# A two-layer decoder in fp32 on one core: the second layer's first query weight is split inside the last layer norm, its value weights later, and four memory pools wait per tile

## The chip, the cores and the metric

The kernel runs on one core of a Trainium2 chip. The metric is device time in microseconds (us) for one execution; less is better. The core has a matrix engine (TensorE, PE in the profile, with its weight loads as PEld), a vector engine (VectorE, DVE), an activation engine (ScalarE, ACT), a general engine (GpSimd, POOL), and a queue that issues most of the loads (SyncE, SP). Each engine executes its own instructions strictly in the order in which they were put there and waits for the others through semaphores.

## What is computed

The input is 512 tokens of 1024 numbers. Layer A is latent attention (8 heads), layer B attention over a window of 128 tokens (16 query heads, 4 key and value heads). After each comes a layer norm, then a multilayer perceptron (MLP) with squared relu and a second layer norm:

```python
for l in range(DEPTH):                       # DEPTH = 2: layer A, then layer B
    if l < n_a:
        y = _mla(x, mla_w_in[l], ...)
    else:
        k_band, v_band = _shared_kv(x, kv_w_shared)
        y = _swa(x, swa_w_q[b], swa_sinks[b], swa_w_o[b], k_band, v_band, rel_bias)
    x = _layernorm(alpha * x + y, ln_mix_g[l], ln_mix_b[l])
    x = _layernorm(alpha * x + _mlp(x, mlp_w_up[l], mlp_w_down[l]), ln_mlp_g[l], ln_mlp_b[l])
```

All of it is fp32. The kernel gets fp32 accuracy from a faster matmul by **splitting** each operand into a high part (a rounding copy) and a low part (the rest), and by adding three products: high by high, high by low, low by high.

## The kernel before, in words

**Stages.** Pools of on-chip memory are opened and closed one after the other: `mla` (layer A's attention), then `xtok` (which stays open), `mlp0`, `swa` (layer B's attention), `mlp1`. Each new pool uses memory that a closed one has left. A tile in such memory may be written only when the work on what lay there is done; with the plain form of `tile_pool` the first use of a new pool waits for all tiles of the old one.

**Weights.** All weights form one list, `stream`, in the order in which the matmuls need them. Each is loaded into one of two `raw` buffers (SP queue, line 140), split on ACT into `wh` (L76) and on DVE or POOL into `wl` (L79), in rings of four tiles each. `weights(name)` hands out the next one and prepares others ahead, up to `state["hold"]`; `prepare(n)` raises that limit by n and prepares at once. Layer B's part of the list begins `w_k`, `w_k`, `w_sq` 0, `w_v`, `w_v`, `w_sq` 1 and so on: two weights for keys, one for the first two query heads, two for values.

**The end of layer A's attention.** `TokMajor.finish` multiplies the heads' outputs by `w_o`, eight weight tiles. The first four give columns 0 to 511 and the last four columns 512 to 1023 of each of the four token tiles `xs[t]`. The residual input is loaded into `xs` (tag `x`) when the `xtok` pool opens (L1105). Each finished token tile goes through `layer_norm` (L391 to L400: aggregate the statistics, `v`, a power on POOL at L375, then two passes over x, L396 and L400).

**The start of layer B.** The last layer norm of the MLP hands its result to `x2`: for each token tile eight PE transposes into two banks (`tr`, two buffers, L411), then an ACT copy `xth` and a DVE subtraction `xtl` of each bank. `begin` computes keys and the first queries in two halves of 256 tokens. In the first half, PE runs `w_k` 0, `w_k` 1, the transposes of token tile 2, four of eight steps of `w_sq` 0, the transposes of token tile 3, the other four steps; in the second half all three again, over token tiles 2 and 3. The keys are split by small 64x256 operations, `skh` on ACT (L1125) and `skl` on DVE (L1126).

**Layer B's heads.** `run_steps` walks 16 heads. For each, PE computes scores; DVE adds the bias and takes the maximum (L1199); ACT takes exponentials (L1207); POOL scales by the reciprocal sum (`p`, L1214 and L1216); PE transposes (L1227, L1229); ACT and DVE split the transposed tile (`pth`, `ptl`); PE multiplies by the values. Per pair of heads the result `o` is split on ACT (`oh`) and POOL (`ol`, L79) for the output matmul with `w_so`. The order in which operations of different heads stand on ACT, DVE and POOL is set by a scheduler, which takes times and priorities into account; the order of PE and of most loads is that of the program (`pe(...)`, `keep_in_program_order`).

Of the kernel before, what the change touches and what calls it, by code (L numbers as in the profile page):

```python
# [8 lines left out]
F32 = mybir.dt.float32  # L9
F32R = mybir.dt.float32r  # L10
# [38 lines left out]
def build(tc, nc, io, out):  # L49
    with ExitStack() as top:  # L50
# [45 lines left out]
        def pin(ins):  # L96

            if pinned[0]:
                pe(ins)
# [286 lines left out]

        def layer_norm(t, gb, dst):

            x = xs[t]
            mv = sp.tile([P, 2], F32, tag="mv", bufs=4, name=nm("mv"))  # L390
            pin(nc.vector.bn_aggr(mv, stats[t]))  # L391
            stats[t] = None
            v = sp.tile([P, 1], F32, tag="v", bufs=8, name=nm("v"))
            pin(nc.vector.tensor_scalar(v, mv[:, 1:2], LN_EPS, None, ALU.add))  # L394
            r = rsqrt_of(v)
            pin(nc.vector.scalar_tensor_tensor(x, x, mv[:, 0:1], gb[:, 0, :], ALU.subtract, ALU.mult))  # L396
            n = 2 if dst is None and t == NT - 1 else 1
            for i in range(n):
                c = slice(i * D // n, (i + 1) * D // n)
                pin(nc.vector.scalar_tensor_tensor(x[:, c], x[:, c], r, gb[:, 1, c], ALU.mult, ALU.add))  # L400
                if dst is None:
                    nc.sync.dma_start(out[t * P : (t + 1) * P, c], x[:, c])
# [22 lines left out]
        class TokMajor:  # L425
# [24 lines left out]

            def finish(self, gb=None, dst=None, early=None):

# [6 lines left out]
                if gb is not None:  # L459
                    gb = gb()  # L460
                    ws = [weights(self.name) for _ in range(4)]
                    for t in range(NT):
# [11 lines left out]
                        with tc.high_priority():  # L474
                            layer_norm(t, gb, dst)
                        if early:
# [71 lines left out]
        def begin(src, chunks):  # L548


            state["hold"] = len(stream)
            ws = [weights(name) for name, _ in chunks]
            for half_ in range(2):
                cols = slice(half_ * 256, half_ * 256 + 256)
                for i, (_, evac) in enumerate(chunks):
# [8 lines left out]
                    if half_ == 0 and i == 1:  # L564
                        with tc.high_priority():
                            src.turn(NT - 2)


# [68 lines left out]
        def mlp(src, gb, dst, mp):  # L637
# [157 lines left out]
            class Hidden:  # L795
# [6 lines left out]
                def of(self, p, k, cols):  # L802
                    n = ((2, 1), (4, 0))[cols.start // 256][k // 4]
                    return b.fac[n][:, p, k % 4, cols.start % 256 : cols.start % 256 + P]

            if dst is not None:
                state["hold"] = first_sq
            TokMajor(Hidden(), add_last, "down").finish(gb, dst, dst and (0, 0, 0, 1))


        ed = dr.tile([SQH, BANDW], F32, name="ed")
        band = dr.tile([SQH, P, 256], F32, name="band")
        with tc.tile_pool(name="mla", bufs=1) as mp:
            const = mp.tile([P, C_ALL], F32, name="const")
            with tc.issue_after(small.ins):
# [3 lines left out]
            sin = const[:, C_SIN : C_SIN + 256].rearrange("p (t d) -> p t d", t=NT)  # L819
            ckv_h = mp.tile([P, 2, S], F32R, name="ckv_h")  # L820
            ckv_l = mp.tile([P, 2, S], F32R, name="ckv_l")
            khh = mp.tile([P, S], F32R, name="khh")
            kll = mp.tile([P, S], F32R, name="kll")
            cq_h = mp.tile([P, 3, S], F32R, name="cq_h")
            cq_l = mp.tile([P, 3, S], F32R, name="cq_l")
            qrot = mp.tile([P, NT, 512], F32, name="qrot")

# [272 lines left out]

        xtok = top.enter_context(tc.tile_pool(name="xtok", bufs=1))

# [4 lines left out]
        x2 = Feat()  # L1107
        with tc.tile_pool(name="mlp0", bufs=1) as mp:
            mlp_pool[0] = mp
# [6 lines left out]

        with tc.tile_pool(name="swa", bufs=1) as mp:
            khh = [mp.tile([P, S], F32R, name=nm("skh")) for _ in range(SKVH)]
# [163 lines left out]
        gb = lambda: load_gb(io["ln_mix_g"][1], io["ln_mix_b"][1])  # L1282
        with tc.tile_pool(name="mlp1", bufs=1) as mp:
            mlp_pool[0] = mp
# [113 lines left out]
```

## Time and profile before

| what | us |
|---|---|
| median of three runs | 1015.11 (1014.65 to 1015.61) |
| the profiled execution, its own time | 1012.41 |
| its span, first to last instruction | 1010.6 |
| PE busy | 991.6 (98%) |
| DVE busy | 767.4 (76%) |
| ACT busy | 555.5 (55%) |
| POOL busy | 232.7 (23%) |

The profiled execution took 1.8 us more than its span (start and end of the program) and 2.7 us less than the median. A row of the timeline gives the start, the duration, the engine, the line of the program, the operation with output and inputs, and in brackets how long the engine had been idle before it and which operation ended that. In a row "wh<-raw", for example, a split's high part is made from a loaded weight. A busy PE is not necessarily PE at its peak; the clock that was granted to it is given for each stretch of time (1.00 is full speed).

### The profile page before, as it was taken

Reading aid. Unit: us, or ns where it says so; the run is one execution under the profiler, and the core shown is the slowest. Engines: PE = TensorE matmul, PEld = TensorE weight load, DVE = VectorE, ACT = ScalarE, POOL = GpSimd, SP = SyncE. Lnnn points to the kernel's source line nnn. Section 1 sums busy time; section 2 is a strip of 40 time slices with the busy share of each in tenths; the row PEclk is TensorE's granted clock in tenths of the full one; section 3 lists DMA queues with packets and bytes.
Section 4 is the critical chain, followed back from the end, with each engine's and each line's share of the span. In section 5 each row is a group of like instructions: output and inputs, shape, how many; then the busy total and the mean of one; then the engine's idle time right before and its main releaser. Section 6 shows DMA issues by size and latency. Waiting matters only on the chain. (4 is left out here: it accounts for less than half of the span.)

```text
span 1010.6 us, 15862 instructions
## 1 busy us (share of the span) xinstructions
PE 991.6 (98%) x6148; PEld 893.4 (88%) x6148; DVE 767.4 (76%) x1231; ACT 555.5 (55%) x847; POOL 232.7 (23%) x204
## 2 busy tenths in 40 slices
PE   8999999999999999999999999999999999999996
PEld 8888887999999999998889888889998999998986
DVE  5588866889769769886695578589896886888756
ACT  5456643467637637646146688446663764665620
POOL 0231101312212211210014674223122032122002
PEclk9999999999999999999999999999999999999999
DMA  7431108397978977963232212247698798798332
GB/s 244 142 99 43 63 22 260 65 218 218 200 167 221 185 178 194 232 117 105 104 104 95 84 65 74 85 124 199 179 217 190 165 221 170 166 265 150 84 125 83
DMA packets 60246, 149.55 MB, mean 148 GB/s; under 512 B 5211, under 2 KB 9740, under 8 KB 60172
## 3 DMA queue, kind: packets, MB, share of 16 engines
q0 software_dynamic: 24320, 58.73, 32.4%
q1 hardware_dynamic: 35852, 89.82, 26.2%
q8 instruction: 48, 0.79, 0.3%
q14 instruction: 26, 0.21, 0.1%
HBM read 146.41 MB, written 4.22 MB: 149 GB/s over the span
## 5 line engine op out<-in xcount | busy, mean ns | idle before, releaser
L103 PE MATMUL mm<-wh,fac 128*128 128x512 f32 (+1 forms) x944 | 293.0, 386 | 0.0
L76 ACT ACTIVATE wh<-wq 128x1024 fp32r<-128x1024 f32 x164 | 173.6, 1060 | 189.5 <-PE mm L103 130.3
L79 DVE TENSOR_TENSOR wl<-wq,wh 128x1024 fp32r<-128x1024 f32 x164 | 199.2, 1221 | 72.6 <-ACT wh L76 71.3
L103 PE MATMUL mm<-xth,wh 128*128 128x256 f32 (+1 forms) x936 | 245.0, 290 | 0.0
L103 PE MATMUL mm<-xth,wl 128*128 128x256 f32 (+1 forms) x808 | 235.0, 291 | 1.5 <-DVE wl L79 1.2
L103 PEld LDWEIGHTS mm<-wh,fac 128*128 128x128 f32 x944 | 176.3, 188 | 35.4 <-DVE fac L79 0.6
L103 PE MATMUL mm<-xtl,wh 128*128 128x256 f32 (+1 forms) x680 | 198.9, 293 | 0.4 <-DVE xtl L79 0.4
L103 PE MATMUL mm<-wl,fac 128*128 128x512 f32 (+1 forms) x472 | 182.6, 387 | 0.0
L103 PEld LDWEIGHTS mm<-xth,wh 128*128 128x128 f32 x936 | 170.3, 192 | 3.0
L103 PEld LDWEIGHTS mm<-xth,wl 128*128 128x128 f32 x808 | 154.8, 192 | 4.4 <-DVE wl L79 2.1
L76 ACT ACTIVATE wh<-raw 128x1024 fp32r<-128x1024 f32 (+4 forms) x85 | 84.3, 997 | 96.4 <-PE mm L103 62.7
L188 POOL DMA_DIRECT2D wq<-in_up x64 | 77.6, 1222 | 246.7 <-DVE wl L79 180.3
L103 PEld LDWEIGHTS mm<-xtl,wh 128*128 128x128 f32 x680 | 130.2, 191 | 3.8 <-DVE xtl L79 0.8
L79 DVE TENSOR_TENSOR wl<-raw,wh 128x1024 fp32r<-128x1024 f32 (+3 forms) x64 | 75.4, 1189 | 40.4 <-ACT wh L76 40.4
L103 PEld LDWEIGHTS mm<-wl,fac 128*128 128x128 f32 x472 | 88.8, 188 | 17.0 <-DVE wl L79 0.5
L188 POOL DMA_DIRECT2D wq<-in_down x48 | 42.0, 874 | 204.8 <-DVE wl L79 201.4
L375 POOL TENSOR_TENSOR rs<-v,half 128x1 f32<-128x1 f32 x24 | 28.8, 1199 | 194.0 <-DVE v L394 156.8
L79 POOL TENSOR_TENSOR wl<-raw,wh 128x1024 fp32r<-128x1024 f32 (+2 forms) x21 | 43.8, 2089 | 79.6 <-ACT wh L76 79.6
L103 PE MATMUL mm<-wh,oh 128*128 128x512 f32 x128 | 51.0, 398 | 0.5 <-ACT wh L76 0.5
L103 PE MATMUL mm<-wh,ol 128*128 128x512 f32 x128 | 50.2, 392 | 1.0 <-POOL ol L79 1.0
L103 PE MATMUL mm<-wl,oh 128*128 128x512 f32 x128 | 50.0, 390 | 0.8 <-DVE wl L79 0.8
L532 DVE TENSOR_TENSOR x<-mm,x 128x512 f32<-128x512 f32 (+1 forms) x53 | 35.6, 676 | 13.8 <-PE mm L103 13.5
(218 smaller groups left out, 1844.3 us busy)
## 6 DMA issues: line engine op xcount, KB each, us to landing
wq<-in_up POOLq DMA_DIRECT2D x64, 512.0 KB, 8.5
wq<-in_down POOLq DMA_DIRECT2D x48, 512.0 KB, 7.9
wq<-in_up SPq DMA_DIRECT2D x32, 512.0 KB, 5.7
raw<-in_down SPq DMA_DIRECT2D x28, 512.0 KB, 6.4
wq<-in_down SPq DMA_DIRECT2D x24, 512.0 KB, 8.2
raw<-in_up SPq DMA_DIRECT2D x16, 512.0 KB, 6.3
raw<-in_w_o SPq DMA_DIRECT2D x8, 512.0 KB, 3.2
raw<-in_w_sq SPq DMA_DIRECT2D x8, 512.0 KB, 3.2
```

The source lines that it names most:

```text
L76: high = nc.scalar.activation(dst_h, src, AF.Copy)
L79: low = (engine or nc.vector).tensor_sub(dst_l, src, f32(dst_h))
L103: pe(nc.tensor.matmul(dst, st, mv, start=first and i == 0, stop=last and i == len(pairs) - 1, **kw))
L188: nc.gpsimd.dma_start(half(a, jp), chunk(*more, jp), accum_op=ALU.add)
L375: nc.gpsimd.tensor_tensor(r, v, half, ALU.pow)
L532: nc.vector.tensor_add(xs[t][:, c], b, xs[t][:, c])
```

## The change

- **The first query weight of layer B** (`w_sq` 0) is no longer loaded into a `raw` buffer. Ahead of the last matmul of layer A's MLP it is loaded into a tile of 128x4x256 numbers with the tag `a12`, a quarter of the MLP's hidden activations that is no longer used by then. Its split is called inside `layer_norm` of the last token tile, between the power on POOL and the first pass over x (`within`), instead of behind that norm.
- **The value weights** come later: `begin` no longer raises the limit at its start. The first `w_v` is prepared behind the first half (`prepare(1)`), the second when it is wanted; the limit is raised at the end.
- **Pools** `xtok`, `mlp0`, `swa` and `mlp1` are opened with `reuse_waits="tile"`: a new tile waits for the old tiles whose memory it takes, not for the whole closed pool.
- **The order of tiles in `mla`** is another, so that other memory lies at the pool's start, where `xtok` will be: `qrot`, `cq_h`, `cq_l` (rotated queries and query latents) come first, in place of `const` (mask and rotary tables), `ckv_h`, `ckv_l` and the rotated keys.

```diff
-        def layer_norm(t, gb, dst):
+        def layer_norm(t, gb, dst, within=None):
...
             r = rsqrt_of(v)
+            if within:
+                within()
             pin(nc.vector.scalar_tensor_tensor(x, x, mv[:, 0:1], gb[:, 0, :], ALU.subtract, ALU.mult))
...
-                            layer_norm(t, gb, dst)
+                            layer_norm(t, gb, dst, within if t == NT - 1 else None)
...
         def begin(src, chunks):
-            state["hold"] = len(stream)
             ws = [weights(name) for name, _ in chunks]
...
+                if half_ == 0:
+                    prepare(1)
+            state["hold"] = len(stream)
...
+            within = None
             if dst is not None:
                 state["hold"] = first_sq
-            TokMajor(Hidden(), add_last, "down").finish(gb, dst, dst and (0, 0, 0, 1))
+                early = mp.tile([P, 4, 256], F32, tag="a12", bufs=1, name=nm("w_sq"))
+                fetchers[first_sq](early.rearrange("p a b -> p (a b)"))
+                within = lambda: prepare(1)
+            TokMajor(Hidden(), add_last, "down").finish(gb, dst, dst and (0, 0, 0, 0), within)
...
         with tc.tile_pool(name="mla", bufs=1) as mp:
+            qrot = mp.tile([P, NT, 512], F32, name="qrot")
+            cq_h = mp.tile([P, 3, S], F32R, name="cq_h")
+            cq_l = mp.tile([P, 3, S], F32R, name="cq_l")
+            ckv_h = mp.tile([P, 2, S], F32R, name="ckv_h")
+            ckv_l = mp.tile([P, 2, S], F32R, name="ckv_l")
             const = mp.tile([P, C_ALL], F32, name="const")
...
-        xtok = top.enter_context(tc.tile_pool(name="xtok", bufs=1))
+        xtok = top.enter_context(tc.tile_pool(name="xtok", bufs=1, reuse_waits="tile"))
...
-        with tc.tile_pool(name="mlp0", bufs=1) as mp:
+        with tc.tile_pool(name="mlp0", bufs=1, reuse_waits="tile") as mp:
...
-        with tc.tile_pool(name="swa", bufs=1) as mp:
+        with tc.tile_pool(name="swa", bufs=1, reuse_waits="tile") as mp:
...
-        with tc.tile_pool(name="mlp1", bufs=1) as mp:
+        with tc.tile_pool(name="mlp1", bufs=1, reuse_waits="tile") as mp:
```

The order of PE's instructions is the same as before, row by row. Three other things move.

**At the end of layer A's attention** no instruction changes its place, but the four loads of `x` on SP do not wait for the same things. Before, the first of them waited for DVE and PE; now the first two wait each for PE alone.

**At the start of layer B, DVE**, from the statistics of the last token tile's norm to the first `xtl` of that tile (`bn`, `mv`, `v`, `x`: the norm; `skl`: a piece of the keys; `wl`: a weight's low part; `xtl`: the low part of transposed x). Before:

```order
L391 BN_AGGR mv_5150<-bn_4965 128x2
L1126 TENSOR_TENSOR skl_5172<-mm_5201,skh_5168 64x256
L394 TENSOR_SCALAR v_5152<-mv_5150 128x1
L396 SCALAR_TENSOR_TENSOR x_1820<-x_1820,mv_5150,gb_4968 128x1024
L1126 TENSOR_TENSOR skl_5172<-mm_5201,skh_5168 64x256
L400 SCALAR_TENSOR_TENSOR x_1820<-x_1820,rs_5154,gb_4968 128x1024
L79 TENSOR_TENSOR wl_5160<-raw_5158,wh_5159 128x1024
L79 TENSOR_TENSOR wl_5185<-raw_5183,wh_5184 128x1024
L1126 TENSOR_TENSOR skl_5173<-mm_5201,skh_5169 64x256
L1126 TENSOR_TENSOR skl_5174<-mm_5234,skh_5170 64x256
L79 TENSOR_TENSOR xtl_1824<-tr_5267,xth_1822 128x4x128
L79 TENSOR_TENSOR xtl_1825<-tr_5274,xth_1823 128x4x128
```

In the changed kernel DVE has, from the same place on:

```order
L394 TENSOR_SCALAR v_5154<-mv_5152 128x1
L79 TENSOR_TENSOR wl_5159<-w_sq_4831,wh_5158 128x1024
L398 SCALAR_TENSOR_TENSOR x_1820<-x_1820,mv_5152,gb_4970 128x1024
L1134 TENSOR_TENSOR skl_5172<-mm_5183,skh_5168 64x256
L1134 TENSOR_TENSOR skl_5174<-mm_5216,skh_5170 64x256
L402 SCALAR_TENSOR_TENSOR x_1820<-x_1820,rs_5156,gb_4970 128x1024
L79 TENSOR_TENSOR xtl_1824<-tr_5249,xth_1822 128x4x128
L1134 TENSOR_TENSOR skl_5172<-mm_5183,skh_5168 64x256
L79 TENSOR_TENSOR xtl_1825<-tr_5256,xth_1823 128x4x128
L1134 TENSOR_TENSOR skl_5174<-mm_5216,skh_5170 64x256
L79 TENSOR_TENSOR wl_5310<-raw_5308,wh_5309 128x1024
L1134 TENSOR_TENSOR skl_5173<-mm_5183,skh_5169 64x256
```

The low part of `w_sq` 0 has moved ahead of both passes over x, and that of the first `w_v` (`raw_5183` before, `raw_5308` now) behind the two `xtl` of token tile 2. The next row, not shown, is the first `xtl` of token tile 3. A piece of `w_k` 1's keys (`skl_5174`) now stands ahead of the norm's second pass. On ACT the first `w_v`'s high part stands behind the two `xth` of token tile 2 and ahead of those of token tile 3. On SP the `w_sq` 0 load has gone to the middle of the last `down` weights, and one bias load and both `w_v` loads follow the second `w_k`.

**Among layer B's last heads, POOL** (`p`: a head's probabilities, scaled in two pieces; `ol`: the low part of a pair's output, which the output matmul needs). Before:

```order
L1216 TENSOR_TENSOR p_6496<-p_6496,ri_6480 128x768
L1214 TENSOR_TENSOR p_6552<-p_6552,ri_6536 128x128
L1216 TENSOR_TENSOR p_6552<-p_6552,ri_6536 128x768
L79 TENSOR_TENSOR ol_5180<-o_6521,oh_5178 128x512
L1214 TENSOR_TENSOR p_6609<-p_6609,ri_6593 128x128
```

And now:

```order
L1224 TENSOR_TENSOR p_6496<-p_6496,ri_6480 128x768
L79 TENSOR_TENSOR ol_5180<-o_6521,oh_5178 128x512
L1222 TENSOR_TENSOR p_6552<-p_6552,ri_6536 128x128
L1224 TENSOR_TENSOR p_6552<-p_6552,ri_6536 128x768
L1222 TENSOR_TENSOR p_6609<-p_6609,ri_6593 128x128
```

The output's low part has moved ahead of the scaling of one head (the last but one). ACT and DVE have some twenty rows in another order around the same place; among them, a bank's `pth` now stands ahead of the last head's exponentials.

More of the change, by code (lines that the diff above doesn't have):

```diff
@@ L449, in part, with finish @@
                     self.evac(t, slice(0, 512), self.b[t])
-            def finish(self, gb=None, dst=None, early=None):
+            def finish(self, gb=None, dst=None, early=None, within=None):
                 for kp in range(4):
@@ L819, in build @@
             sin = const[:, C_SIN : C_SIN + 256].rearrange("p (t d) -> p t d", t=NT)
-            ckv_h = mp.tile([P, 2, S], F32R, name="ckv_h")
-            ckv_l = mp.tile([P, 2, S], F32R, name="ckv_l")
             khh = mp.tile([P, S], F32R, name="khh")
             kll = mp.tile([P, S], F32R, name="kll")
-            cq_h = mp.tile([P, 3, S], F32R, name="cq_h")
-            cq_l = mp.tile([P, 3, S], F32R, name="cq_l")
-            qrot = mp.tile([P, NT, 512], F32, name="qrot")
             def scratch():
```

## The prediction

> **What bounds the kernel now.** I read the page first, then the timeline of PE alone for every row with an idle time ahead of it, then the timelines of SP, ACT, DVE and POOL around those rows.
>
> ```profile
> span 1010.6 us, 15862 instructions
> ...
> PE 991.6 (98%) x6148; PEld 893.4 (88%) x6148; DVE 767.4 (76%) x1231; ACT 555.5 (55%) x847; POOL 232.7 (23%) x204
> ```
>
> ```profile
> 1000.00:1010.60 10.60, 2.94 (x25) 2.73 (x23) 6.10 (x11) 0.00 (x0) 2.20 (x2) 0.80 0.26 99
> ```
>
> PE is the bound: it is idle for 1010.6 − 991.6 = 19.0 us in all, and 10.60 − 2.94 = 7.7 us of that is the end of the program (the second row is the last stretch of a table of windows; PE's busy time is the second number). The order of PE's instructions does not change, so the change can only shorten waits of PE, or add some. These are the waits over 0.5 us behind the first 10 us of the program:
>
> ```profile
> 170.10 0.50 PE L103 MATMUL mm<-wh,oh 128*128 128x512 f32 x1 [0.53 <-ACT wh L76]
> 171.36 0.50 PE L103 MATMUL mm<-wl,oh 128*128 128x512 f32 x1 [0.76 <-DVE wl L79]
> 523.13 0.39 PE L103 MATMUL mm<-xth,wl 128*128 128x256 f32 x1 [1.17 <-DVE wl L79]
> 525.77 1.25 PE L411 MATMUL tr<-ident,x 128*128 128x128 f32 x8 [1.18 <-DVE xtl L79]
> 620.24 0.30 PE L1227 MATMUL tr<-ident,p 128*128 128x128 f32 x1 [2.28 <-DVE ptl L79]
> 633.99 0.50 PE L103 MATMUL mm<-wh,ol 128*128 128x512 f32 x1 [0.95 <-POOL ol L79]
> ```
>
> Together 6.87 us, at four places: the last `w_o` weight (1.29), the start of layer B (2.35), two of layer B's heads (2.28 and 0.95). Both MLPs, most of the span, have no such wait, so a pool that waits per tile has nothing to win inside them.
>
> **The change part by part.**
>
> *Term 1, the loads of x.*
>
> ```profile
> 79.18 52.74 SPq L140 DMA_DIRECT2D raw<-in_w_o  x6
> 154.57 2.46 SPq L1105 DMA_DIRECT2D x<-in_x  x4
> 158.40 0.33 SPq L140 DMA_DIRECT2D raw<-in_w_o  x1
> 160.07 0.38 SPq L140 DMA_DIRECT2D raw<-in_w_o  x1
> ```
>
> ```profile
> 164.57 1.06 ACT L76 ACTIVATE wh<-raw 128x1024 fp32r<-128x1024 f32 x1 [6.14 <-DMA raw<-in_w_o]
> 168.99 1.06 ACT L76 ACTIVATE wh<-raw 128x1024 fp32r<-128x1024 f32 x1 [3.35 <-DMA raw<-in_w_o]
> ```
>
> ```profile
> 129.00 0.39 PE L103 MATMUL mm<-cq_h,wl 128*128 128x512 f32 x1
> ```
>
> ```profile
> 161.45 0.69 DVE L529 SCALAR_TENSOR_TENSOR x<-x,mm 128x512 f32<-128x512 f32 x1 [1.76 <-PE mm L103]
> ...
> 162.81 0.69 DVE L529 SCALAR_TENSOR_TENSOR x<-x,mm 128x512 f32<-128x512 f32 x1
> ```
>
> ```profile
> raw<-in_w_o SPq DMA_DIRECT2D x8, 512.0 KB, 3.2
> ```
>
> Before, SP has issued six `w_o` loads by 79.18 + 52.74 = 131.9 and then stands until 154.57, when the old pool is free; only then come four x loads of 512 KB, and they share the DMA engines with the last two `w_o` loads. These land after 6.1 us (158.40 to 164.5) and 8.9 us (160.07 to 168.95); the median of all eight is 3.2. The last one makes PE wait. With the new order x takes the memory of `qrot` and `cq`. The last matmul on `cq` is at 129.00, and `qrot` is last read before that in program order. So x can be issued at 131.9 and has landed some 20 us before the last two `w_o` loads are issued; those times stay, since they hang on raw buffers that DVE frees. Even at 6.1 us the last `w_o` lands at 166.2. Its split also needs the ring tile that PE frees: the first evacuation is at 161.45, the next three follow 1.36 apart (162.81 − 161.45), so it is free at 165.5. High part by 166.2 + 1.06 = 167.3, low part 1.2 later (half of the 2.35 that two take, in term 2) at 168.5; PE wants the tile at 170.10 − 0.53 = 169.57. Both waits go: **−1.29**. Bounds: 0 (x stays late) and −1.29. I take the whole, because the only load ahead of x in SP's order has its row. What the loads now run beside is attention, where no load is waited for.
>
> *Term 2, the start of layer B.*
>
> ```profile
> 517.15 1.06 ACT L76 ACTIVATE wh<-raw 128x1024 fp32r<-128x1024 f32 x1 [3.67 <-DMA raw<-in_w_sq]
> ```
>
> ```profile
> 512.64 1.22 DVE L79 TENSOR_TENSOR wl<-raw,wh 128x1024 fp32r<-128x1024 f32 x1
> ...
> 517.61 0.26 DVE L391 BATCH_NORM_AGGREGATE mv<-bn 128x2 f32<-128x24 f32 x1
> 518.50 0.41 DVE L1126 TENSOR_TENSOR skl<-mm,skh 64x256 fp32r<-64x256 f32 x1 [0.62 <-ACT skh L1125]
> 518.84 0.14 DVE L394 TENSOR_SCALAR v<-mv 128x1 f32<-128x1 f32 x1
> ...
> 520.65 1.29 DVE L400 SCALAR_TENSOR_TENSOR x<-x,rs,gb 128x1024 f32<-128x1024 f32 x1
> 521.86 2.35 DVE L79 TENSOR_TENSOR wl<-raw,wh 128x1024 fp32r<-128x1024 f32 x2
> ...
> 525.04 1.27 DVE L79 TENSOR_TENSOR xtl<-tr,xth 128x512 fp32r<-128x512 f32 x2
> ```
>
> ```profile
> 518.95 0.38 ACT L1125 ACTIVATE skh<-mm 64x256 fp32r<-64x256 f32 x1 [0.48 <-DVE skl L1126]
> ```
>
> ```profile
> 520.57 0.28 PE L103 MATMUL mm<-xth,wl 128*128 128x256 f32 x1
> ...
> 528.41 0.28 PE L103 MATMUL mm<-xtl,wh 128*128 128x256 f32 x1
> ```
>
> Before, DVE makes the low part of `w_k` 0 early (512.64) and two more (521.86, 2.35) behind the norm; PE waits for the first of them, then for the `xtl` behind both. In the new order I walk DVE with these durations (`wl` 1.18, a pass over x 1.28, `xtl` 0.64, `skl` 0.42):
> - statistics done 517.87; `v` no longer stands behind an `skl` that waited 0.62: done 518.0; `wl` of `w_sq` 0 (loaded long before, so its high part no longer waits 3.67 for the load) 519.15; first pass 520.4; `skl` 520.85.
> - The next `skl` belongs to `w_k` 1, whose last matmul ends at 520.57 + 0.28 = 520.85; with 0.4 for its `skh`, DVE waits until 521.3 and ends at 521.7. Second pass 523.0: one us *later* than before (520.65 + 1.29 = 521.94).
> - `xtl` 523.65, `skl` 524.05, `xtl` 524.7, `skl` 525.1, `wl` of `w_v` 526.3, `skl` 526.7, first `xtl` of tile 3 527.35.
>
> PE: both halves of token tile 3's transposes wait for a bank, at 523.65 and 524.7 (before: 525.77 for the first). But the second half's second matmul needs the `xtl` of 527.35: 527.4, where before it ran at 528.41. So of 2.35 us of waits 1.0 goes and 1.35 turns into new, shorter waits: **−1.0**. Queued behind the moved `wl` are the norm and the `skl`; who waits for those is PE, as walked. Bounds: −2.35 (all waits go) and, since the norm ends later, +1.06 (that delay reaches PE undiminished). I take the walk, nearer to the first.
>
> The earlier load costs one more issue on SP among `down` weights, which are split when PE frees a ring tile and not when they land; the later `w_v` 1 is split, as before, when PE frees its tile. Both 0; without that cover, the 3.2 of a landing.
>
> *Term 3, the last heads.*
>
> ```profile
> 630.88 0.40 POOL L1214 TENSOR_TENSOR p<-p,ri 128x128 f32<-128x128 f32 x1 [3.67 <-DVE ri L1213]
> ...
> 632.67 1.27 POOL L79 TENSOR_TENSOR ol<-o,oh 128x512 fp32r<-128x512 f32 x1
> ```
>
> ```profile
> 630.04 0.64 ACT L76 ACTIVATE oh<-o 128x512 fp32r<-128x512 f32 x1
> ```
>
> ```profile
> 635.74 0.27 PE L1227 MATMUL tr<-ident,p 128*128 128x128 f32 x1
> ```
>
> Before, POOL scales head 14 from 630.88 and only then makes the `ol` for which PE waits until 633.94. Its input is ready at 630.04 + 0.64 = 630.7. Now `ol` comes first: 630.7 + 1.27 = 632.0, ahead of PE's wish at 633.99 − 0.95 = 633.04. Head 14's `p` takes 1.8 (630.88 to 632.67) and ends at 633.8; its transposes come at 635.74 − 0.95 = 634.8, so they don't wait. The wait goes: **−0.95**. Bounds: −0.95, and +1.3 (the length of `ol`, if head 14 turns late). ACT's and DVE's new order there puts nothing in front of this chain longer than one bank's `pth`, about 0.5, so I take −0.95.
>
> *Kept.* The wait of 2.28 at 620.24 hangs on DVE rows that keep their order: 0.
>
> **The sum.** −1.29 − 1.0 − 0.95 = **−3.24 us**. Against the profiled execution: 1010.6 − 3.2 = 1007.4 of span, 1012.41 − 3.24 = 1009.2 of time. The median of the runs stands 2.7 above that execution; I carry the difference over to it: 1015.11 − 3.24 = **1011.9**. About 0.2% (2.0 us) is what a measurement of this kernel can tell from no change: 1013.1 is the edge.
>
> **A clock rule, weighed.**
>
> ```profile
> 620.00:622.00 2.00, 1.75 (x9) 1.42 (x10) 1.91 (x7) 1.62 (x4) 1.51 (x2) 0.64 0.06 23
> 622.00:624.00 2.00, 2.00 (x11) 2.00 (x11) 1.75 (x3) 2.00 (x9) 1.28 (x1) 0.51 0.00 0
> ```
>
> ```profile
> 624.63 0.27 PE L1227 MATMUL tr<-ident,p 128*128 128x128 f32 x1
> ...
> 627.26 0.40 PE L103 MATMUL mm<-wh,oh 128*128 128x512 f32 x1
> ```
>
> After the wait of 2.28 us the granted clock (third number from the end) falls to 0.64 and 0.51, as much as a half clock for (0.36 + 0.49) × 2 / 0.5 = 3.4 us. One head's transposes, mix and scores take 624.63 − 620.24 = 4.39 there and 627.26 − 624.63 = 2.63 for the next head: the drop costs 1.76. [...]
>
> **The rivals.**
> - *Term 3 doesn't come*: the new order of DVE and ACT delays the chain of head 14 or 15 by as much as `ol` gains. For it: some twenty rows move. Against: PE's wish has 1.0 us to spare. 1015.11 − 2.29 = 1012.8.
> - *Only the x loads count*: at layer B the later norm eats the gain (the middle of its bounds), and term 3 fails. 1015.11 − 1.29 = 1013.8, no measurable change. This is also the case in which the early split does not do what it says.
> - *The clock*: with less waiting around it, or another phase, the drop at 620 stays away: a further −1.76, 1010.1. For it: one drop follows one wait in this trace, while the two waits at layer B, as long together, were followed by none. [...]
> - *Slower*: the first `w_v` blocks ACT and DVE. Its high part stands ahead of token tile 3's `xth` on ACT and its low part ahead of the `xtl` on DVE; whatever it comes late, PE's second half comes late.
>
> ```profile
> 516.22 7.28 SPq L140 DMA_DIRECT2D raw<-in_w_v  x2
> ```
>
> Before, the second `w_v` load was issued only at 516.22 + 7.28 = 523.5, when its raw buffer came free. By my walk the first may land until 523.2; from 523.2 + 3.24 = 526.4 on the kernel is slower than before. If it is held as the second was and lands 6.1 us later (as one `w_o` in term 1), at 529.6, the time is 1015.11 + 3.2 = 1018.3. Against: its buffer is that of `w_k` 0, split by 512.64 + 1.22 = 513.9.
>
> **How the numbers follow.** Forecast 0.50; term 3 missing 0.16 (0.10 below the edge, 0.06 above); only x 0.18; clock 0.10; slower 0.06. Faster 0.50 + 0.10 + 0.10 = 0.70, same 0.06 + 0.18 = 0.24, slower 0.06. The range leaves out only the slower case and the far ends of the unknown costs: from the clock's 1010.1 to the x-only 1013.8, and on both sides the 0.5 by which the three runs lie about their median: 1009.6 to 1014.3. That holds the middle of term 2's bounds too.
>
> **What would show it.** The x loads issued near 132 and no PE wait on `w_o` near 170; the `w_sq` 0 high part made before the last norm, PE's waits near 522 to 526 (shifted by 1.3) adding up to some 1.3 and the second half starting 1.0 earlier relative to 170; no wait on `ol`, with the 2.28 wait still there. Wrong would be: x still behind 150, a wait in place of the one on `ol`, a new wait over 0.5 us elsewhere, or a slow clock at another place.

## The result

| | median, us | range, us | runs |
|---|---|---|---|
| before | 1014.88 | 1014.12 to 1015.61 | 4 |
| changed | 1009.7 | 1007.21 to 1009.99 | 4 |

The changed kernel takes 0.9946 of the time (95% interval 0.993 to 0.9962): 5.2 us less, where 3.24 was forecast. A second comparison, among the experiments, gives 5.9 us.

### The profile after

The page of the changed kernel: PE has the same number of instructions and the same busy time as before; what the change took away is idle time.

```profile
span 1008.1 us, 15853 instructions
...
PE 991.7 (98%) x6148; PEld 894.4 (89%) x6148; DVE 767.9 (76%) x1231; ACT 556.7 (55%) x847; POOL 232.7 (23%) x204
```

SP's queue around the loads of x, changed kernel. They are issued 21 us earlier than before, and the last two `w_o` loads no longer stand directly behind them:

```profile
133.06 2.05 SPq L1113 DMA_DIRECT2D x<-in_x  x4
159.47 0.33 SPq L140 DMA_DIRECT2D raw<-in_w_o  x1
...
160.84 0.38 SPq L140 DMA_DIRECT2D raw<-in_w_o  x1
```

These are all of PE's waits over 0.3 us behind the program's first 10 us. No row waits on `w_o` near 170, and none on `ol` near 634; the 2.28 us stay (the line numbers of the heads are 8 higher in the changed file). At layer B's start two waits of together 2.35 have become three of together 1.62:

```profile
523.10 0.66 PE L413 MATMUL tr<-ident,x 128*128 128x128 f32 x4 [0.42 <-DVE xtl L79]
524.27 0.66 PE L413 MATMUL tr<-ident,x 128*128 128x128 f32 x4 [0.52 <-DVE xtl L79]
527.16 0.39 PE L103 MATMUL mm<-xtl,wh 128*128 128x256 f32 x1 [0.68 <-DVE xtl L79]
619.07 0.33 PE L1235 MATMUL tr<-ident,p 128*128 128x128 f32 x1 [2.28 <-DVE ptl L79]
```

### The two executions, stage by stage

Waits that a view lists are not yet time lost. What is lost is read by cutting each execution at the same matmuls and comparing starts. Five cuts serve here, and the last row of PE: a matmul of layer A's queries, the first transposes of layer A's MLP, those of layer B, layer B's first scores, the first transposes of layer B's MLP. Before, then changed:

```profile
59.05 0.39 PE L103 MATMUL mm<-cq_h,wl 128*128 128x512 f32 x1
178.05 0.60 PE L619 MATMUL tr<-ident,x 128*128 128x128 f32 x4
502.26 0.60 PE L411 MATMUL tr<-ident,x 128*128 128x128 f32 x4
539.81 0.22 PE L103 MATMUL mm<-skh,q 128*128 128x128 f32 x1
667.38 0.38 PE L619 MATMUL tr<-ident,x 128*128 128x128 f32 x2
1002.66 0.28 PE L103 MATMUL mm<-wh,fac 128*128 128x256 f32 x1
```

```profile
60.12 0.39 PE L103 MATMUL mm<-cq_h,wl 128*128 128x512 f32 x1
177.32 0.49 PE L623 MATMUL tr<-ident,x 128*128 128x128 f32 x3
501.79 0.38 PE L413 MATMUL tr<-ident,x 128*128 128x128 f32 x2
538.65 0.22 PE L103 MATMUL mm<-skh,q 128*128 128x128 f32 x1
664.87 0.38 PE L623 MATMUL tr<-ident,x 128*128 128x128 f32 x2
1000.14 0.28 PE L103 MATMUL mm<-wh,fac 128*128 128x256 f32 x1
```

The differences: start +1.07, layer A's attention −1.80, its MLP +0.26, layer B's start −0.69, its heads −1.35, the last MLP −0.01; together −2.52, which is, to 0.01, how far the two profiled executions differ (1012.41 and 1009.88). The +1.07 is no work of the change: from 8 to 12 us this execution had a slow clock (0.56 and 0.59, the third number from the end); in the profiled execution of before it was 1.00 there. In the twelve other executions below, this first cut lies between 58.27 and 60.01 with either kernel.

```profile
8.00:10.00 2.00, 1.89 (x7) 1.66 (x8) 0.39 (x1) 0.12 (x1) 0.00 (x0) 0.56 1.01 362
10.00:12.00 2.00, 2.00 (x10) 2.00 (x10) 1.03 (x1) 1.61 (x3) 0.00 (x0) 0.59 1.02 375
```

Without it the mechanisms gave 3.6 us in these two executions, near the forecast. The medians differ by 5.2 to 5.9. So the open question was not what the change does, but why the median gains some 2 us more than the pair of traces.

### The profile page after: what moved, and what is told of

It reads as the page before. It is cut to its first block, busy times and chain, and to the rows that moved or that the text cites. A ratio compares the mean times of both kernels' runs of the same rounds, so it can differ in the third digit from the quotient of the medians.

```text
span 1008.1 us, 15853 instructions
## 1 busy us (share of the span) xinstructions
PE 991.7 (98%) x6148; PEld 894.4 (89%) x6148; DVE 767.9 (76%) x1231; ACT 556.7 (55%) x847; POOL 232.7 (23%) x204
## 4 chain that ended last, share of the span: by engine, by line
PE 75%; DVE 3%; DMA 1%; issue 1%; ACT 0%; POOL 0%; POOLq 0%; DVEq 0%
PE mm L103 69%; PE tr L103 5%; DMA wq<-in_up 1%; DVE wl L79 1%; PE tr L1235 1%; DVE x L402 1%; PE tr L1237 1%; DVE xtl L79 0%; PE tr L623 0%; POOL rs L375 0%; DVE uv L594 0%; DVE bn L528 0%; ACT wh L76 0%; PE tr L413 0%; POOLq L1402 0%
```

## Experiments

Theory: the price of the three terms differs from execution to execution, and the profiled execution of before was a cheap one. Rival: the terms are constants, and the change does something else that the traces don't show.

All times are medians. The kernels of one group were compared with runs of the kernel before in the same group: 1014.68 in the first (`same`, `after_again`, `x_only`, `lb_only`), 1015.86 in the second (`old_order` to `fill620`; one of its eleven runs took 3478 us, for no known reason), 1014.85 in the last (`ol_first`, `same_b`, `same_c`, `both`).

### Unchanged kernels, for more executions

The kernel before four times in all (the profiled one and three more), the changed one twice. No edit.

> The kernel before, unchanged, timed against itself. The profile of before has one drop of the granted clock (620 to 624), that of the changed kernel two (8 to 12 and 620 to 624), yet the medians differ by 5.2 us and the two profiled executions by 2.5. Theory (drops come by chance of phase, about 2 us each, and the profiled execution of before happened to have one fewer than its timed runs): the times form groups about 1.5 to 2.7 us apart, near 1012.4 with a mean clock of 0.996 and near 1014.5 to 1015.6 with 0.993 to 0.995. Rival (the drops belong to the kernel; executions scatter for another reason): the mean clock is the same in all runs, 0.996, and so is the profile's single drop.

> The changed kernel, unchanged, on this chip. Theory: like the kernel before, groups by clock, near 1007.2 at 0.998 (one drop) and near 1009.8 at 0.995 (two drops); in executions with equal clocks it is 3.2 to 3.9 us ahead of the kernel before, by the three waits that its trace shows shortened. Rival: the change itself keeps a drop away, so that it is ahead by about 5 us at any clock.

> The kernel before, unchanged, for one more execution. Theory (the profiled execution with which the sum was made had short waits and few clock drops): the two waits on w_o near 170 add up to more than 1.29, in 1.6 to 2.3; the wait on ol is above 0.95, in 1.3 to 1.7; the waits at layer B stay 2.35; a slow clock in one or two further places besides 620, at the start or at layer B. Rival (the waits are constants of the kernel and the executions differ elsewhere): 1.29 and 0.95 within 0.1.

> The kernel before, unchanged, for one more execution. Theory and rival as for the other unchanged one: waits on w_o near 170 of 1.6 to 2.3 in sum and on ol of 1.3 to 1.7 by the theory, 1.29 and 0.95 by the rival. Of five unchanged starts of layer B (this one, the last, and three before them) one or two show a slow clock there, if it comes by chance of phase as in one of three so far.

Measured: `same` 1014.99 (0.9992, interval 0.9981 to 1.0004); `after_again` 1008.81 (0.9937, 0.9921 to 0.9952); `same_b` 1016.31 and `same_c` 1016.59, one run each. `same_b` at the two places of terms 1 and 3, and the clock behind the first:

```profile
171.83 0.50 PE L103 MATMUL mm<-wh,oh 128*128 128x512 f32 x1 [1.41 <-ACT wh L76]
173.09 0.79 PE L103 MATMUL mm<-wl,oh 128*128 128x512 f32 x1 [0.76 <-DVE wl L79]
...
637.93 0.50 PE L103 MATMUL mm<-wh,ol 128*128 128x512 f32 x1 [2.08 <-POOL ol L79]
```

```profile
172.00:174.00 2.00, 1.24 (x3) 0.83 (x4) 1.94 (x2) 1.81 (x2) 0.00 (x0) 0.67 0.44 170
174.00:176.00 2.00, 2.00 (x6) 1.52 (x6) 0.70 (x2) 1.36 (x2) 1.35 (x1) 0.50 0.88 245
```

The waits on `w_o` are 0.53 + 0.76 in the profiled execution, 1.44 + 0.76 in `same`, 1.41 + 0.76 in `same_b`, 1.75 + 0.76 in `same_c`. In the last two the clock falls to 0.50 behind them, in the others it stays at 1.00. The wait on `ol` is 0.95, 1.63, 2.08 and 1.45. So these waits are not constants, and the execution with which the sum was made had the shortest of both: the theory stands on this point (the 2.51 of `same_c` and the 2.08 lie above the ranges it gave). The waits at layer B were 2.35 to 2.41 in all four, with a clock of 1.00 behind them; a slow one came in one of the five old starts meant there, that of `x_only` (below).

The groups of times that the first expectation named don't show: in its group the kernel before took 1013.06 to 1016.40 at a mean clock of 0.996 (12 runs) and 1013.09 to 1017.34 at 0.994 (10 runs). Nor was the clock the same in all runs, as its rival had it: it went from 0.991 to 0.999. The theory of the second expectation misses too: at 0.996 the changed kernel was 5.5 us ahead (2 runs against 12), and not 3.2 to 3.9. Its rival's 5 us is nearer, and the reason it gave holds in part: a drop near 170 came in two of the six executions with a late x (0.50 in `same_b` and `same_c`; layer A's attention took 121.30 and 121.86 us there) and in none of the eight with an early one (117.14 to 117.40 us).

### Parts of the change alone

`x_only`: the new order of `mla`'s tiles, and `xtok` alone waiting per tile. `lb_only`: the early `w_sq` 0 and the late value weights alone, with the old pools and the old order of tiles.

```diff
 x_only
+            qrot = mp.tile([P, NT, 512], F32, name="qrot")
+            cq_h = mp.tile([P, 3, S], F32R, name="cq_h")
...
-        xtok = top.enter_context(tc.tile_pool(name="xtok", bufs=1))
+        xtok = top.enter_context(tc.tile_pool(name="xtok", bufs=1, reuse_waits="tile"))
 lb_only
+                early = mp.tile([P, 4, 256], F32, tag="a12", bufs=1, name=nm("w_sq"))
+                fetchers[first_sq](early.rearrange("p a b -> p (a b)"))
+                within = lambda: prepare(1)
...
+                if half_ == 0:
+                    prepare(1)
+            state["hold"] = len(stream)
```

> Only the tile order of the first attention's pool and the per-tile waits of the pool that holds x; layer B as before. Theory (three separate terms): x is issued near 133, no wait on w_o at 170, PE 1.3 to 1.6 us earlier from there on; the waits at 523, 525, 620 and 634 stay as in the kernel before; 1.3 to 1.6 us less at equal clock. Rival (the gain is given back at layer B, which is bound by something else): below 0.5 us.

> Only the early split of the first query weight and the later value weights; pools and tile order as before, so x is loaded at 154. Theory: the two waits of 0.53 and 0.76 at 170 stay, the layer-B waits become about 0.4, 0.5 and 0.7, the wait on ol at 634 goes, since the scheduler's order of the last heads follows from this part; 0.8 + 1.26 = about 2.0 us less at equal clock. Rival (the per-tile waits of the attention pool are what makes the new order work): under 1 us, with a wait of over 0.5 us at 515 to 530 on the pool.

Measured: `x_only` 1012.36 (0.9977, 0.9965 to 0.9988), −2.3; `lb_only` 1011.68 (0.9965, 0.9952 to 0.9979), −3.0. The order of layer B's last heads comes with `lb_only`: the scheduler makes it out of the other weights. The parts add up to 5.3, within the whole's 5.2 to 5.9, and each brings about one us more than its waits in the profiled execution of before (1.29; and 1.0 + 0.95).

`x_only` keeps layer B's start as it was, and there shows in one execution what chance does: the same waits as before, but now with half a clock behind them (the row of PE, then the clock around it). What decides it is left open (the slow clock, below).

```profile
525.24 1.97 PE L411 MATMUL tr<-ident,x 128*128 128x128 f32 x8 [1.18 <-DVE xtl L79]
```

```profile
524.00:526.00 2.00, 0.82 (x5) 0.77 (x5) 1.94 (x5) 0.76 (x2) 0.00 (x0) 0.75 0.79 293
526.00:528.00 2.00, 2.00 (x11) 2.00 (x10) 1.48 (x4) 1.33 (x3) 0.00 (x0) 0.50 0.53 188
```

### `ol_first`: term 3 alone

The kernel before, with head 14's scaling of `p` held behind the `ol` of the sixth pair on POOL. No other row of any engine moves.

```diff
-                nc.gpsimd.tensor_mul(p[:, 0, P:], p[:, 0, P:], ri[:, 0:1].broadcast_to([P, P]))
...
+                if h == 14:
+                    later.append(scale)
+                else:
+                    scale()
...
+                    if h == 11:
+                        with behind(pair):
+                            later[0]()
```

> The kernel before with one pair of rows exchanged on POOL: the ol of the sixth pair of heads stands ahead of head 14's scaling of p, as the change has it; every other row of every engine stays. Theory (term 3 was read from an execution with a short wait): the wait on ol goes, and the time falls by the mean of the three waits seen in unchanged executions, (0.95 + 1.63 + 1.54) / 3 = 1.4 us, with 1.0 to 1.7 as bounds. Rival 1 (the profiled execution's 0.95 is the price): -0.95. Rival 2 (the wait is only moved to head 14's transposes or to the next ol): a new wait of 0.5 us or more within 634 to 650, and no change of the time within 0.5 us. The stretch from layer B's first scores to the transposes of its output, 127.6 to 128.1 in the unchanged executions, would be 126.2 to 126.7 by the theory.

Measured: 1012.94 (0.998, 0.9967 to 0.9993), −1.9. The wait on `ol` is gone, and in its place stands a shorter one, on head 14's transposes:

```profile
636.01 0.30 PE L1234 MATMUL tr<-ident,p 128*128 128x128 f32 x1 [0.88 <-DVE ptl L79]
```

The stretch of the heads is 126.99 us in this one execution, 0.7 above the mean of 126.3 of the change and 0.8 below the 127.77 of before (table below). Theory and second rival each hold in part. The row on POOL is worth about 0.8 by itself; the rest of term 3 needs the new order of DVE and ACT, the only other thing that differs there, which I had counted only as a risk.

### `old_order`: is it the tile order or the waits per tile?

The changed kernel with `mla`'s tiles in the old order.

```diff
-            qrot = mp.tile([P, NT, 512], F32, name="qrot")
-            cq_h = mp.tile([P, 3, S], F32R, name="cq_h")
...
+            cq_h = mp.tile([P, 3, S], F32R, name="cq_h")
+            cq_l = mp.tile([P, 3, S], F32R, name="cq_l")
+            qrot = mp.tile([P, NT, 512], F32, name="qrot")
```

> The changed kernel with MLA's tiles allocated in the old order again; all four pools still wait per tile, and every engine's instructions keep their order. Theory (the order of the tiles puts x into memory that is free early): x issued near 155 again, the two waits on w_o near 170 come back with 1.3 to 2.3 us, no other wait changes: 1008.8 + 1.3 to 2.3 = 1010.1 to 1011.1. Rival (the pools that wait per tile do it, whatever the order): x stays near 132, no wait on w_o, 1008.8.

Measured: 1008.47 (0.9931, 0.9916 to 0.9946), as the changed kernel. The theory falls: the loads of x are issued between its two times, and no wait on `w_o` is left.

```profile
144.03 1.75 SPq L1113 DMA_DIRECT2D x<-in_x  x4
```

The waits per tile are enough; the new order of tiles moves x another 11 us ahead, and nothing waits for that. The new order without the waits per tile was not run.

### `wv_later`: the wait that the change left at layer B

The first `w_v` is split behind the last `xtl` and no longer ahead of it.

```diff
-                split(dst.hs[n][:, :, tk], dst.ls[n][:, :, tk], pt)
+                state["turned"] = split(dst.hs[n][:, :, tk], dst.ls[n][:, :, tk], pt)
...
                 if half_ == 0:
-                    prepare(1)
+                    with behind(state["turned"]):
+                        prepare(1)
```

> The changed kernel with the split of the first w_v weight held behind token tile 3's splits, where it no longer stands ahead of their low parts on DVE. Theory (term 2's remaining 1.6 us of new waits is in part this split): the wait of 0.68 near 527 goes, the two of 0.42 and 0.52 near 523 stay, 1008.8 - 0.7 = 1008.1. Rival (the weight is then late for its own matmuls): a new wait on wl or wh of w_v near 529 takes its place, 1008.8 or more.

Measured: 1007.56 (0.9921, 0.9907 to 0.9935). Layer B's start is 35.92 us long, 0.94 less than in the changed kernel; the wait of 0.68 has gone, and the two others stand as they were:

```profile
522.76 0.65 PE L413 MATMUL tr<-ident,x 128*128 128x128 f32 x4 [0.42 <-DVE xtl L79]
523.93 0.66 PE L413 MATMUL tr<-ident,x 128*128 128x128 f32 x4 [0.52 <-DVE xtl L79]
```

No wait on `w_v` takes its place. This is the version to keep: its median is below both kernels' (1008.81 and 1009.7 for the change, in other groups of runs); that it beats the change rests on the stage's 0.94 in the trace, since the two intervals overlap.

### `so3_pool` and `fill620`: the 2.28 us that stay

The first gives the low part of the fourth `w_so` weight to POOL, since DVE made it ahead of head 11's chain. The second puts seven matmuls on zeros into PE's wait; they write a bank that the next mix clears.

```diff
 so3_pool
-POOL_O, POOL_SO = (0, 2), (0, 1, 2)
+POOL_O, POOL_SO = (0, 2), (0, 1, 2, 3)
 fill620
+                if h == 11:
+                    spare_bank.append(bank())
+                    group(spare_bank[0], [(zeros[:, :P], zeros[:, P:])] * 7)
...
-                b = bank()
+                b = spare_bank[0] if h == 10 else bank()
```

> The changed kernel with the low part of the fourth output weight of layer B's attention made on POOL and not on DVE, in whose row it stands ahead of head 11's chain. PE's order is the same. Theory: the wait of 2.28 near 619 falls by the length of that low part, to about 1.1; if the clock then stays up there too, a further 1.3 to 1.8: 1007.6, or 1005.8 to 1006.3. Rival (POOL's 4th low part makes POOL late for the next ol or for the scaling of p): a new wait on POOL of 0.5 or more within 620 to 640, 1008.8 or more.

> The changed kernel with seven matmuls on zeros on PE ahead of head 11's transposes, so that PE works through the 2.28 us in which it now waits; they write a bank that the next mix clears. Theory (the idle time brings the slow clock, and the slow clock costs time of its own): no window with a granted clock under 0.99 near 616 to 624, and 1.3 to 1.8 us less, 1007.0 to 1007.5. Rival 1 (the drop there is no matter of this idle time): it stays, 1008.8. Rival 2 (the drop is made up by shorter waits behind it): the drop goes and the time stays 1008.8. The matmuls may end up to 0.3 us behind the wait, which would be added.

Measured, `so3_pool`: 1010.7 (0.9949, 0.9933 to 0.9964). That is 2.2 us above `old_order` in the same group; against the change itself the intervals overlap, but the heads take 128.15 us in its trace in place of 126.3. DVE, freed of the weight, waits for ACT's query instead, and PE's wait keeps its length; a second one comes behind it (a row of DVE, then rows of PE):

```profile
615.46 0.69 DVE L1179 TENSOR_TENSOR q<-mm,q 64x512 fp32r<-64x512 f32 x1 [1.22 <-ACT q L1178]
```

```profile
618.86 0.30 PE L1235 MATMUL tr<-ident,p 128*128 128x128 f32 x1 [2.28 <-DVE nb L1211]
...
624.03 0.30 PE L1235 MATMUL tr<-ident,p 128*128 128x128 f32 x1 [0.63 <-DVE ptl L79]
```

Theory and rival both miss: the weight on DVE was covered, and by the rows it is ACT for which the chain waits. What costs the time behind it stays open, since the edit is not the weight alone: the scheduler also put many rows of DVE and some of ACT and POOL in another order from 617 us on.

`fill620`: 1008.71 (0.9934, 0.9918 to 0.995). The windows 618 to 622 of `after_again`, then of `fill620` (the second number is PE's busy time, the third from the end the granted clock):

```profile
618.00:620.00 2.00, 1.93 (x10) 1.61 (x11) 1.91 (x6) 1.39 (x3) 1.35 (x1) 0.59 0.04 8
620.00:622.00 2.00, 2.00 (x12) 2.00 (x12) 1.59 (x3) 2.00 (x9) 1.12 (x1) 0.56 0.00 0
```

```profile
618.00:620.00 2.00, 1.78 (x15) 1.60 (x15) 1.91 (x6) 1.79 (x4) 1.31 (x1) 1.00 0.00 0
620.00:622.00 2.00, 1.97 (x19) 1.79 (x17) 1.94 (x6) 2.00 (x9) 1.28 (x1) 1.00 0.00 0
```

With PE at work the clock stays at 1.00 (0.59 and 0.56 without the matmuls), and the heads take 125.42 us in place of 126.3: the theory holds in the trace, with 0.9 in place of 1.3 to 1.8. The median does not show it and is where the second rival had it; its interval is as wide as 3 us, so whether the gain is real there stays open.

### `both`: `wv_later` and `fill620` together

The two diffs above in one kernel.

> The changed kernel with the split of the first w_v weight held behind token tile 3's splits and with the seven matmuls on zeros ahead of head 11's transposes, the two changes that gained something in their traces. If they add up: the first took 0.93 us from layer B's start and 1.0 to 1.6 of the ratio's per mille, the second 0.9 us from the heads; 0.9918 to 0.9925 of the kernel before, about 1007. If the slow clock that the matmuls keep away at 620 comes at another place instead: as the first alone, 0.992.

Measured: 1007.62 (0.9924, 0.9904 to 0.9944), as `wv_later` alone. The trace keeps both gains (35.91 and 125.43 us in the two stages), with a clock of 1.00 throughout 616 to 624. The median shows nothing of the second, but an interval of 4 us does not tell 0.992 for the first alone from 0.9918 to 0.9925 for both: whether the gains add up stays open.

### All executions, stage by stage

Each number is the difference of the starts of two of the rows named above; a column holds the executions in which that stage is as before, and those in which it is as changed. Where an experiment's own edit moves rows in a stage, its execution is left out there.

| stage | as before | mean | as changed | mean | difference |
|---|---|---|---|---|---|
| layer A's attention (term 1) | 119.00, 119.92, 121.30, 121.86, 119.86, 119.62 | 120.26 | 117.14 to 117.40, eight | 117.22 | −3.04 |
| its MLP | 324.21 to 325.18, six | 324.77 | 324.20 to 325.66, eight | 324.66 | −0.1 |
| layer B's start (term 2) | 37.55, 37.57, 37.61, 37.61, 38.30, 38.82 | 37.91 | 36.85 to 36.86, six | 36.86 | −1.05 |
| layer B's heads (term 3) | 127.57, 128.08, 127.56, 127.80, 127.83 | 127.77 | 126.51, 126.53, 126.22, 126.30, 126.10 | 126.33 | −1.44 |

The first number of each list "as before" is the profiled execution of the prediction. The three terms add up to −5.5 us, which is what the medians show (−5.2 and −5.9). The rival, something else that the change does, is not needed. These are means of four to eight single executions, and term 1's old values alone spread over 2.9 us.

## Why the prediction was right in kind and short in size

**Term 1** was right in its mechanism (x near 133, both waits gone) and mis-sized: −1.29 forecast, −1.80 between the two profiled executions, −3.04 in the mean. The first half us is a fault of reading. Rows of before on both sides of the two waits:

```profile
168.95 0.39 PE L103 MATMUL mm<-wl,oh 128*128 128x512 f32 x1
169.18 0.39 PE L103 MATMUL mm<-wh,ol 128*128 128x512 f32 x1
...
171.69 0.40 PE L103 MATMUL mm<-wh,ol 128*128 128x512 f32 x1
171.92 0.39 PE L103 MATMUL mm<-wh,oh 128*128 128x512 f32 x1
```

Undisturbed, these matmuls start 0.23 apart (169.18 − 168.95), though each is 0.39 long: they overlap. From 169.18 to 171.69 there are three steps, 0.68 undisturbed, and they took 2.51: 1.83 were lost where the two idle times listed add up to 1.29, since an idle time counts only from the end of the last matmul. The other 1.2 us are the executions: the waits were 2.17 to 2.51 in three others of before, and in two of those half a clock followed (in `lb_only` and `ol_first`, which also load x late, they were 1.82 and 2.14). My 1.29 was named as one end of the bounds; the cost lay outside them.

The walk also had the last `w_o` load too early. I let it land at most 6.1 us after its issue, with its low part ready 1.1 us ahead of PE. In the changed kernel it was issued at 160.84 and split from 168.21 on:

```profile
168.21 1.06 ACT L76 ACTIVATE wh<-raw 128x1024 fp32r<-128x1024 f32 x1 [3.88 <-DMA raw<-in_w_o]
```

Its low part was ready at 170.53, and PE's first matmul on it started at 170.70. Over the eight executions with an early x this load took 7.0 to 7.5 us from issue to landing (8.8 to 10.0 in the six with x beside it), and the low part came 0.06 to 0.46 us ahead of its use. So the wait went by a narrow margin, and the loads of x were only part of what made this load slow.

**Term 2** was right as a walk. It put PE's waits at 523.65, 524.7 and 527.4; moved by the 0.47 us that the changed execution was ahead at 502, they came at 523.57, 524.74 and 527.63. Against the four old starts of 37.55 to 37.61 it gave −0.7 for −1.0. The mean is −1.05, because two starts of the old kind took longer; that it lies beside the forecast −1.0 is luck. In `x_only` it was the slow clock (0.50). In `ol_first` it was a wait of 1.96 in place of 1.18: the first `w_v` landed late, so that ACT split it from 522.78 on (521.51 in the profiled execution), and DVE's low part of it stands ahead of the `xtl` for which PE waits. The change takes it out of that place:

```profile
522.78 1.06 ACT L76 ACTIVATE wh<-raw 128x1024 fp32r<-128x1024 f32 x1 [3.34 <-DMA raw<-in_w_v]
...
526.66 1.25 PE L411 MATMUL tr<-ident,x 128*128 128x128 f32 x8 [1.96 <-DVE xtl L79]
```

**Term 3** came, so that the rival without it fell: −1.35 in the two executions and −1.44 in the mean, for −0.95. Here too the listed idle time is short of the loss. The two matmuls ahead of the wait at 633.99:

```profile
632.41 0.40 PE L103 MATMUL mm<-wh,oh 128*128 128x512 f32 x1
632.65 0.39 PE L103 MATMUL mm<-wl,oh 128*128 128x512 f32 x1
```

The next came 1.34 behind the second (633.99 − 632.65) and not 0.24: 1.10 lost. `ol_first` adds that POOL's row alone is not all of it.

**Kept** was right: 2.28 before, 2.28 after.

**The step that failed** is "The median of the runs stands 2.7 above that execution; I carry the difference over to it". It takes the 2.7 for a constant that has nothing to do with the change. But 1.26 of it (120.26 − 119.00) stands in the stage of term 1, 0.36 in that of term 2 and 0.20 in that of term 3, and there the change takes it away with the rest. Those 1.82 us are most of what the sum fell short by. The rest is the terms' own price: between the two profiled executions the three stages gave 3.84 (1.80 + 0.69 + 1.35) for 3.24, terms 1 and 3 more than forecast and term 2 less. With the mean prices the same sum gives 1015.11 − 5.5 = 1009.6.

**The rivals.** The clock's 1010.1 is near the measured time, but not by its mechanism: the slow clock at 620 stayed in the profiled changed kernel (0.50 from 619.21 to 622.63) and in `after_again`, `lb_only` and `wv_later`, which have its heads and no matmuls in the wait (down to 0.56, 0.73 and 0.70 in the windows read). Kept away by `fill620` it was worth 0.9 in the trace, and not 1.76. Of the signs named as wrong, one came, a slow clock at another place (8 to 12 us). It is no mark of the change: the profiled execution of `after_again`, the changed kernel once more, had a mean clock of 0.996, as that of before, and `same`, the kernel before, one of 0.994. The waits of 0.52 and 0.68 at layer B are those of term 2's walk; the three there add up to 1.62 where the walk had 1.35. The slower case did not begin. DVE of the changed kernel around the split of the first `w_v`:

```profile
523.52 0.69 DVE L79 TENSOR_TENSOR xtl<-tr,xth 128x512 fp32r<-128x512 f32 x1
...
524.69 1.23 DVE L79 TENSOR_TENSOR wl<-raw,wh 128x1024 fp32r<-128x1024 f32 x1
...
526.41 0.69 DVE L79 TENSOR_TENSOR xtl<-tr,xth 128x512 fp32r<-128x512 f32 x1
```

It stands ahead of token tile 3's first `xtl`, as the rival had it, but no idle time is listed ahead of it: the weight was there. What it costs by standing there is the 0.94 that `wv_later` gets back.

**The slow clock.** The drop near 620 lasts 3.41 us in both profiled executions. In the rows below the second number is PE's busy time and the third from the end the granted clock: first the 3.4 us ahead of the drop and the drop itself in the profiled execution of before, then the same place in `same_b`.

```profile
617.14:620.56 3.42, 1.14 (x10) 0.96 (x10) 3.32 (x14) 3.37 (x12) 0.87 (x2) 1.00 0.43 153
620.56:623.97 3.41, 3.40 (x17) 3.04 (x16) 3.10 (x6) 3.05 (x11) 2.23 (x2) 0.50 0.00 0
```

```profile
616.00:620.00 4.00, 4.00 (x26) 3.46 (x25) 3.46 (x14) 2.90 (x5) 3.07 (x3) 1.00 0.37 142
620.00:624.00 4.00, 1.90 (x17) 1.69 (x15) 3.74 (x12) 3.95 (x14) 0.37 (x2) 1.00 0.38 128
624.00:628.00 4.00, 3.60 (x29) 3.25 (x30) 3.81 (x11) 3.70 (x12) 2.74 (x3) 1.00 0.01 3
```

In the first, PE is busy for 1.14 of the 3.42 us ahead of the drop (1.13 of 3.41 in the profiled changed kernel). In `same_b` PE is idle for 2.10 us between 620 and 624, and no drop comes. In `same_c` it is idle for 2.13 us there, and the drop comes (0.58 from 624 to 628). With the waits of terms 1 and 2 it is the same. Behind nearly equal waits on `w_o` there was a drop in `same_b` (1.41 + 0.76) and none in `same` (1.44 + 0.76); behind nearly equal ones at layer B there was one in `x_only` (1.15 + 1.18) and none in the profiled execution of before (1.17 + 1.18). So the length of a wait alone does not tell whether a drop follows, and what does is left open: that a phase decides it, as the prediction and the expectations have it, was the author's estimate, and no run here is enough to show it. What the runs show in its place is that the drop came in some executions of a kernel and stayed away in others.

Where no drop came, in `same_b`, the wait on `ol` was 2.08 and the stage 127.56, as long as with a drop (127.57 in the profiled execution): that fits a chain over POOL that sets the end of the stage in either case, so that what a slow clock costs PE is taken out of the later wait. A sum of drop and wait would count the same time twice there.

## What to carry to other kernels

Read the price of a wait from the starts of the instructions around it and not from its listed idle time, above all where instructions overlap (here they start 0.23 us apart and are 0.39 long). Take that price from several executions before carrying a difference over to the median: the wait for a load that ran beside others was no constant here (1.29 to 2.51 us on `w_o`), and the execution at hand had the shortest. Whether a wait is followed by a slow clock is also read from several executions: behind the 2.28 us one came in both profiled executions and none in `same_b`. Let a pool wait per tile first; the order of the tiles may then be worth nothing, as in `old_order` (1008.47).

## What the runs showed of the hardware

- The clock fell to 0.50 behind some waits of PE and stayed at 1.00 behind others of nearly the same length: it fell behind 1.41 + 0.76 us on `w_o` in `same_b`, not behind 1.44 + 0.76 in `same`; behind 1.15 + 1.18 at layer B in `x_only`, not behind 1.17 + 1.18 in the profiled execution of before; behind the 2.28 us in both profiled executions (for 3.41 us each), not in `same_b`. Behind `w_o` a drop cost about 1.4 us (layer A's attention took 121.30 in `same_b`, 119.92 in `same`, with waits of 2.17 and 2.20). With seven matmuls on zeros in the 2.28 us (0.68 of idle time stayed), a clock of 1.00 followed in both kernels that had them (`fill620`, `both`).
- A load of 512 KB (the last `w_o`) landed in different times in different executions of one program: its split began 8.9 us behind its issue in the profiled execution, 9.8 in `same_b` (160.93 to 170.72) and 10.0 in `same_c` (160.23 to 170.27), all with the loads of x beside it. Without them it still took 7.0 to 7.5 us, and PE never waited for it.
